# The features of x in a hybrid decoder trunk: the array made 64 bytes longer, with two starts inside it

## The chip, the cores and the metric

The kernel runs on one core of a Trainium2 chip. The metric is device microseconds of one execution. The core has TensorE (PE, with its weight loads shown as PEld), VectorE (DVE), ScalarE (ACT), GpSimd (POOL) and SyncE (SP). Its on-chip memory has 128 partitions; a tile's place is a byte offset that is the same in every partition.

## The reference

A trunk of two layers on 256 tokens of width 2048, in float32. Layer 0 normalises x, projects it with one matrix of 6144 columns, feeds a gated linear recurrence (RG-LRU) and a gated outer-product recurrence (HGRN2), projects the result, and ends with a squared-ReLU MLP of width 8192. Layer 1 has windowed attention in the place of the recurrences, and the same MLP.

```
proj = h @ w_in                                   # layer 0, one combined projection
mixed = concat([lru, hg]);   h = h + mixed @ w_out
h = h + square(relu(rms_norm(h) @ w1)) @ w2       # both layers
qkv = (h @ w_qkv)                                 # layer 1
h = h + dilated_attention(...) @ w_o
```

## The kernel before, in words

**Products in parts.** Every float32 operand is split into a high part (rounded to the chip's short float32 format, fp32r) and a low part (the remainder). A product is three matmuls: high by high, high by low, low by high. Weights arrive as tiles of 128 x 2048 (1 MB); `Weights` (lines 101 to 117) makes `hi` by a ScalarE copy (line 112) and `lo` by a VectorE subtraction (line 113). There are three buffers each of `raw`, `hi` and `lo`, used in turn. Weights that are sums or differences of two tiles go through `t1`/`t` and `s` (lines 138 to 166), which is how the later stages save matmuls.

**The array of x's features.** `bufa` (line 62) has 16 blocks of 128 features; block k holds 256 columns of the high part (one per token) and then 256 columns of the low part, so 512 words or 2048 bytes a block and 32768 bytes a partition. Layer 0 fills it while the weights of the first projection arrive (`fetch_first`, line 182). Two kinds of reader follow in layer 0. `tokens` (line 311, called by `tokens_group`, line 338) takes 128 x 128 slices of the features as the stationary operand and streams 512 columns of weights past them; the steps `v0 k0 v1 k1` of the order in line 1076 do this. `project` (line 346, by way of `direct`, line 230) takes a 128 x 128 slice of weights as the stationary operand and streams 256 columns of features; the steps `h`, `x` and `y` do this (`hgrn`, `lru_in`, `lru_out`).

**Later stages.** From layer 0's MLP on, `to_features` (line 668) writes the features of the new x to `bufa`, and `blocks` (line 605) reads slices of it through `feature` (line 597) as the stationary operand, with 512 columns of weights streamed. The other stationary arrays are `bufb`, `formx` and `formh`.

**Order.** All matmuls are tied into one chain (`mm`, line 195), so TensorE's order is that of the code. A scheduler places the rest; loads are fetched two units ahead (`unit`, line 185).

**Where tiles lie.** Pools are laid out one after the other. These are the byte offsets in a partition that the built program has, and where they fall in a block of 2048 and of 128 bytes:

| tile | bytes | offset | within 2048 | within 128 |
|---|---|---|---|---|
| constants (`cst`), `tab_`, `ones` | | 4224 to 6944 | | |
| `xall` (x by tokens) | 16384 | 6944 | 800 | 32 |
| `bufa` | 32768 | 23328 | 800 | 32 |
| `raw` (first of 3) | 8192 | 56096 | 800 | 32 |
| `hi` (first of 3) | 8192 | 80672 | 800 | 32 |
| `lo` (first of 3) | 8192 | 105248 | 800 | 32 |
| `bufb` | 32768 | 132384 | 1312 | 32 |
| `formx` | 16384 | 165152 | 1312 | 32 |
| `t1` / `s` | 8192 | 181536 / 189728 | 1312 | 32 |
| `formh` | 16384 | 197920 | 1312 | 32 |

A weight slice of 128 columns is 512 bytes and one of 512 columns is 2048 bytes; a stationary slice of features is 512 bytes. So before the change the two operands of every fp32r matmul start at offsets that differ by a multiple of 512 bytes.

Of the kernel before, what the change touches and what calls it, by code (L numbers as in the profile page):

```python
# [11 lines left out]
F32R = mybir.dt.float32r  # L12
# [8 lines left out]
P = 128  # L21
S = 256
D = 2048
KB = D // P
# [18 lines left out]
def trunk_kernel(ctx, tc, begin, xtok, cols, tab, masks, pos, fin, w_in, w_gate, w_out, w_qkv, w_o, w1, w2, out):  # L43
# [3 lines left out]
    act = pool("act")  # L47
# [11 lines left out]

    xall = act.tile([P, KB * S], F32, name="xall")  # L60
    xres = xall.rearrange("p (j d) -> p j d", j=2)
    bufa = act.tile([P, KB, 2 * S], F32R, name="bufa")

    units = []
    made = {}
# [15 lines left out]
    for step in ORDER.split():  # L81
        src, first, n = where[step[0]]
# [85 lines left out]
    def fetch_first():  # L168
        r = opening.tile([P, 14, WIDE], F32, name="first")
        e = wraw.tile([P, 2048], F32, name="raw")[:, :2 * WIDE].rearrange("p (k s) -> p k s", s=WIDE)  # L170
        homes = [r[:, k] for k in range(14)] + [e[:, k] for k in range(2)]
        nc.sync.dma_start(r[:, 0, :S], begin[:, 0, :S])
        nc.sync.dma_start(r[:, 0, S:], begin[:, 0, S:])
        for k in range(1, 4):
            nc.sync.dma_start(r[:, k], begin[:, k])
        for k in range(4, 16, 2):
            nc.sync.dma_start(r[:, k:k + 2] if k < 14 else e, begin[:, k:k + 2])
        for u in range(4):
            at[0] += 1
            w = made[u] = Weights(None, 0)  # L180
            for k in range(4 * u, 4 * u + 4):
                split_to(bufa[:, k], homes[k][:, :S], col("nmix0", k))
                w.split((k - 4 * u) * 512, 512, homes[k][:, S:])

    def unit(src, i):
# [52 lines left out]
    def split_to(dst, src, gain=None):  # L238
        if gain is None:
            h, l = dst[..., :S], dst[..., S:]  # L240
            A.copy(h, src)
            V.tensor_tensor(l, src, h.bitcast(F32), OP.subtract)
        else:
            A.activation(dst[:, :S], src, AF.Copy, scale=gain)
            V.scalar_tensor_tensor(dst[:, S:], src, gain, dst[:, :S].bitcast(F32),  # L245
                                   op0=OP.mult, op1=OP.subtract)

    c_ = cst.tile([P, NCOL], F32, name="c_")
    col = lambda n, i=0, w=1: c_[:, COLS[n][0] + i:COLS[n][0] + i + w]
# [86 lines left out]
        return ps  # L336

    def tokens_group(src, i0, rt=None, by_k=False, name="vg"):
        ps = tokens(src, i0, bufa, by_k)
        v = vgs.tile([P, 2, 512], F32, name=name)  # L340
        with urgent():
            for j in range(2):
                A.activation(v[:, j], ps[j], AF.Copy, scale=1.0 if rt is None else rt[:, j:j + 1])
        return v

    def project(src, i, mov):
        w = unit(src, i)
        p = pmm.tile([P, 512], F32, name="p")
        direct(p, w, [(k, mov[:, k], k == 0, k == KB - 1) for k in range(KB)])
        return p  # L350
# [85 lines left out]
    def hgrn(hd, vg, gg):  # L436
        u0 = 20 + (hd // 4) * 16 + (hd % 4) * 2
        oml = omlb[:, hd:hd + 1]
        qk = wk.tile([P, 2 * S], F32, name="qk", bufs=3)
        qp, kq = qk[:, :S], qk[:, S:]  # L440
        p = project(w_in, u0, bufa)
        z = normed(p, "hz", 4)
        lut(qp, z, AF.Sigmoid)
        V.scalar_tensor_tensor(qp, z, oml, qp, op0=OP.mult, op1=OP.mult)
        p = project(w_in, u0 + 1, bufa)
        z = normed(p, "hz", 4)
        f = wk.tile([P, S], F32, name="f", bufs=3)
        lut(f, z, AF.Sigmoid)
        lut(kq, z, AF.Sigmoid, scale=-1.0)
        V.tensor_scalar(f, f, oml, lb[:, hd:hd + 1], op0=OP.mult, op1=OP.add)  # L450
        pd = psc.tile([P, 2, P], F32, name="pd", bufs=1)
        for j in range(2):
            js = slice(j * P, j * P + P)
            T.matmul(pd[:, j], kq[:, js], qp[:, js], start=True, stop=True)  # L454
        st = wk.tile([P, 3, P], F32, name="st", bufs=3)
        V.tensor_tensor(st[:, :2], pd, ident[:, None, :].to_broadcast([P, 2, P]), OP.mult)
        stf = st[:, :2].rearrange("p a b -> p (a b)")
        V.tensor_tensor(qp, qp, f, OP.mult)
        c = 1
        tot = f  # L460
        while c <= 128:
            pl = psc.tile([P, 2, 64], F32, name="pl", bufs=2)
            if c == 128:
                plf = pl.rearrange("p j c -> p (j c)")
                T.matmul(plf, kq[:, :P], qp[:, P:], start=True, stop=True)  # L465
                A.copy(st[:, 2], plf)
                break
            for j in range(2):
                js = slice(j * P, j * P + P)
                T.matmul(pl[:, j], kq[:, js], halves(qp[:, js], c, True), start=True, stop=True)  # L470
            if c <= 16:
                lv = LEVELS.index(c)
                V.copy_predicated(halves(stf, c, True), msk[:, lv].rearrange("p (n c) -> p n c", c=c),
                                  pl.rearrange("p j (n c) -> p (j n) c", c=c))
            elif c == 32:
                for n in range(2):
                    ps_ = slice(64 * n, 64 * n + 32)
                    A.copy(st[ps_, :2, 64 * n + 32:64 * n + 64], pl[ps_, :, 32 * n:32 * n + 32])
            else:
                A.copy(st[:64, :2, 64:], pl[:64])  # L480
            n = S // (2 * c)
            tt = tot.rearrange("p (n two) -> p n two", two=2)
            both = bass.AP(tensor=qk.tensor, offset=qk.offset + c,
                           ap=[list(qk.ap[0]), [S - c, 2], [2 * c, n], [1, c]])
            fac = bass.AP(tensor=tot.tensor, offset=tot.offset,
                          ap=[list(tot.ap[0]), [1, 2], [2, n], [0, c]])
            V.tensor_tensor(both, both, fac, OP.mult)
            nt = wk.tile([P, n], F32, name=f"tot{n}", bufs=2)
            V.tensor_tensor(nt, tt[:, :, 0], tt[:, :, 1], OP.mult)
            tot = nt  # L490
            c *= 2
        vs = slice((hd % 4) * P, (hd % 4) * P + P)
        po = psc.tile([P, 2, P], F32, name="po", bufs=1)
        T.matmul(po[:, 0], st[:, 0], vg[:, 0, vs], start=True, stop=True)
        T.matmul(po[:, 1], st[:, 2], vg[:, 0, vs], start=True, stop=False)  # L495
        T.matmul(po[:, 1], st[:, 1], vg[:, 1, vs], start=False, stop=True)  # L496
        o = wk.tile([P, 2, P], F32, name="ho", bufs=2)
        hs = wk.tile([P, 2], F32, name="hs", bufs=2)
        for j in range(2):
            A.activation(o[:, j], po[:, j], AF.Square, accum_out=hs[:, j:j + 1])  # L500
        V.tensor_scalar(hs, hs, 1.0 / P, EPS, op0=OP.mult, op1=OP.add)
        hr = wk.tile([P, 2], F32, name="hr", bufs=2)
        rsqrt(hr, hs, 2)
        for j in range(2):
            V.scalar_tensor_tensor(o[:, j], po[:, j], hr[:, j:j + 1], gg[:, j, vs], op0=OP.mult, op1=OP.mult)
        pt = psc.tile([P, 2, P], F32, name="pt", bufs=1)
        for j in range(2):
            T.transpose(pt[:, j], o[:, j], ident)
        split_to(bufb[:, 8 + hd], pt.rearrange("p j c -> p (j c)"), col("gn", hd))
# [1 line left out]
    xc = wk.tile([P, 8, S], F32, name="xc", bufs=1)  # L511

    def lru_in(b):
        p = project(w_in, b, bufa)
        xp = wk.tile([P, S + 4], F32, name="xp", bufs=1)
        V.memset(xp[:, :4], 0.0)
        scaled(p, xp[:, 4:])
        A.activation(xc[:, b], xp[:, 4:], AF.Identity, bias=col("conv_b", b), scale=col("conv_w", 24 + b))
        for i in range(3):
            V.scalar_tensor_tensor(xc[:, b], xp[:, 1 + i:1 + i + S], col("conv_w", 8 * i + b), xc[:, b],  # L520
                                   op0=OP.mult, op1=OP.add)
        split_to(bufb[:, b], xc[:, b])
# [24 lines left out]
            V.tensor_tensor_scan(xc[:, b], gr[:, m], xc[:, b], 0.0, op0=OP.mult, op1=OP.add)  # L547

    def lru_out(b):
        p = project(w_in, 8 + b, bufa)  # L550
        y = tmp.tile([P, S], F32, name="z")
        scaled(p, y)
        q = wk.tile([P, S], F32, name="q", bufs=1)
        A.activation(q, y, AF.Square, scale=math.sqrt(0.044715))
        V.scalar_tensor_tensor(q, q, 1.0, y, op0=OP.add, op1=OP.mult)
        lut(q, q, AF.Sigmoid, scale=2.0 * math.sqrt(2.0 / math.pi))
        V.tensor_tensor(y, y, q, OP.mult)
        V.tensor_tensor(y, y, xc[:, b], OP.mult)
        split_to(bufb[:, b], y)
# [470 lines left out]
    for i, what in enumerate(ATTENTION):  # L1030
# [12 lines left out]
        else:  # L1043
            q, k = queries_keys(i, ((1, 0),) if not i else ())
# [24 lines left out]

LAST = 2  # L1070
EARLY = 12
BOUNDARY = 56
PRIO = 150
URGENT = 400
# [114 lines left out]
```

## Time and profile before

| what | value |
|---|---|
| median of 3 runs | 2133.09 us (2132.8 to 2133.53) |
| the profiled execution's own time | 2133.06 us |
| its span, first to last instruction | 2131.3 us |
| PE busy | 2120.9 us, 100% of the span, 10542 matmuls |
| PEld busy | 1797.6 us, 84% |
| DVE busy | 1788.8 us, 84% |
| ACT busy | 1378.2 us, 65% |
| DMA | 488.71 MB, mean 229 GB/s |
| granted TensorE clock | 0.999 |

A row of the groups reads: line, engine, operation, output and inputs by the program's names, shape, count, then busy us and the mean ns of one, then the engine's idle time just before them. PE matmuls overlap in the record, since each is shown from its start to the end of its results; the distance from one start to the next is what a matmul costs a full engine.

### The profile page before, as it was taken

To read this page: it belongs to the slowest core of one execution; us is meant where nothing else is said; L and a number is where in the kernel's file an instruction comes from. 1 tells how busy PE (TensorE), PEld (TensorE's weight loads), DVE (VectorE), ACT (ScalarE), POOL (GpSimd) and SP (SyncE) were. 2 spreads that over 40 slices of the span, in tenths; PEclk is the share of its full clock that TensorE was granted. 3 is DMA by queue.
4 is the path that set the end of the run, shared out by engine and by line. 5 is a ranking of instruction groups with operands and counts; after the bars stand their busy time and mean duration, and the time that the engine had idled before them with its cause. 6 is when DMAs were issued, how large, how long until landed. Compare 5 with 4: busy or idle time off the path is not lost.

```text
span 2131.3 us, 26730 instructions
## 1 busy us (share of the span) xinstructions
PE 2120.9 (100%) x10542; PEld 1797.6 (84%) x10542; DVE 1788.8 (84%) x1962; ACT 1378.2 (65%) x1543; POOL 66.8 (3%) x85
## 2 busy tenths in 40 slices
PE   9999999999999999999999999999999999999998
PEld 8989998888888888888888888888888888888886
DVE  7777888888888888888988797788897888888887
ACT  7445565776476567567666777776756765755764
POOL 0000000000000000000000000000000000000000
PEclk9999999999999999999999999999999999999999
DMA  8444446686777677677887767777767768777773
GB/s 336 162 162 158 161 148 224 206 269 233 227 237 253 230 240 253 227 241 231 270 279 218 241 199 247 254 247 228 246 237 253 236 212 269 238 234 227 271 225 146
DMA packets 69806, 488.71 MB, mean 229 GB/s; under 512 B 7808, under 2 KB 8320, under 8 KB 11952
## 3 DMA queue, kind: packets, MB, share of 16 engines
q1 hardware_dynamic: 58176, 410.96, 51.1%
q0 software_dynamic: 11216, 75.70, 18.3%
q8 instruction: 82, 1.34, 0.3%
q14 instruction: 44, 0.36, 0.0%
q10 hardware_dynamic: 288, 0.34, 0.0%
HBM read 482.78 MB, written 4.19 MB: 228 GB/s over the span
## 4 chain that ended last, share of the span: by engine, by line
PE 99%; DVE 0%; ACT 0%; DMA 0%; issue 0%; ACTq 0%; DVEq 0%; POOLq 0%
PE p L196 62%; PE po L196 14%; PE pd L196 13%; PE pt L196 5%; PE pl L199 2%; PE pl L470 1%; PE pl L196 0%; PE pd L199 0%; DMA ppi<-in_pos 0%; PE pd L454 0%; DVE lo L113 0%; ACT hi L112 0%; PE pl L465 0%; PE po L495 0%; PE po L496 0%
## 5 line engine op out<-in xcount | busy, mean ns | idle before, releaser
L113 DVE TENSOR_TENSOR lo<-raw,hi 128x2048 fp32r<-128x2048 f32 (+2 forms) x397 | 787.1, 1991 | 164.5 <-ACT hi L112 159.4
L112 ACT CAST hi<-raw 128x2048 fp32r<-128x2048 f32 (+2 forms) x397 | 657.3, 1671 | 335.1 <-PE p L196 175.5
L196 PE MATMUL p<-hi,bufa 128*128 128x512 f32 x1488 | 482.0, 394 | 0.0
L196 PE MATMUL p<-hi,bufb 128*128 128x512 f32 x1128 | 363.1, 391 | 0.0
L196 PEld LDWEIGHTS p<-hi,bufa 128*128 128x128 f32 x1488 | 279.2, 188 | 57.3 <-DVE bufa L245 0.5
L113 DVE TENSOR_TENSOR lo<-s,hi 128x2048 fp32r<-128x2048 f32 (+1 forms) x164 | 285.9, 1753 | 28.6 <-ACT hi L112 27.6
L112 ACT CAST hi<-s 128x2048 fp32r<-128x2048 f32 (+1 forms) x164 | 242.7, 1480 | 98.2 <-DVE s L164 54.2
L196 PE MATMUL p<-lo,bufa 128*128 128x512 f32 x744 | 287.6, 390 | 0.2 <-DVE lo L113 0.2
L196 PEld LDWEIGHTS p<-hi,bufb 128*128 128x128 f32 x1128 | 211.7, 188 | 43.7
L196 PE MATMUL p<-lo,bufb 128*128 128x512 f32 x564 | 219.5, 389 | 0.0
L196 PE MATMUL p<-bufa,hi 128*128 128x256 f32 x1024 | 193.2, 287 | 0.0
L196 PEld LDWEIGHTS p<-lo,bufa 128*128 128x128 f32 x744 | 139.9, 188 | 28.0 <-DVE lo L113 0.7
L196 PEld LDWEIGHTS p<-bufa,hi 128*128 128x128 f32 x1024 | 161.2, 191 | 0.2
L196 PE MATMUL p<-bufa,lo 128*128 128x256 f32 x512 | 146.5, 286 | 0.0
L112 ACT CAST hi<-t 128x2048 fp32r<-128x2048 f32 x41 | 78.5, 1914 | 99.6 <-PE p L196 91.1
L113 DVE TENSOR_TENSOR lo<-t,hi 128x2048 fp32r<-128x2048 f32 x41 | 94.0, 2292 | 55.4 <-ACT hi L112 55.0
L196 PEld LDWEIGHTS p<-lo,bufb 128*128 128x128 f32 x564 | 105.9, 188 | 21.5
L196 PE MATMUL p<-hi,formh 128*128 128x512 f32 x368 | 120.7, 391 | 0.0
L196 PE MATMUL p<-hi,formx 128*128 128x512 f32 x352 | 115.9, 390 | 0.0
L196 PE MATMUL po<-hi,bufb 128*128 128x512 f32 x320 | 103.7, 390 | 0.0
L196 PEld LDWEIGHTS p<-bufa,lo 128*128 128x128 f32 x512 | 98.0, 191 | 0.0
L164 DVE TENSOR_TENSOR s<-s,raw 128x1024 f32<-128x1024 f32 x82 | 96.4, 1216 | 0.1
(319 smaller groups left out, 3292.4 us busy)
## 6 DMA issues: line engine op xcount, KB each, us to landing
raw<-in_w SPq DMA_DIRECT2D x224, 1024.0 KB, 6.1
raw<-in_w_in SPq DMA_DIRECT2D x44, 1024.0 KB, 4.8
raw<-in_w_qkv SPq DMA_DIRECT2D x42, 1024.0 KB, 6.9
t<-in_w SPq DMA_DIRECT2D x32, 1024.0 KB, 4.9
t<-in_w POOLq DMA_DIRECT2D x32, 1024.0 KB, 8.7
s<-in_w POOLq DMA_DIRECT2D x17, 1024.0 KB, 8.4
raw<-in_w_out SPq DMA_DIRECT2D x15, 1024.0 KB, 4.8
raw<-in_w_o SPq DMA_DIRECT2D x14, 1024.0 KB, 7.7
```

The source lines that it names most:

```text
L112: a = A.copy(h, w)
L113: v = V.tensor_tensor(l, w, h.bitcast(F32), OP.subtract)
L164: V.tensor_tensor(s, s, held["c"][:, at:at + 1024], OP.add)
L196: chain[:] = [after(T.matmul(*args, **kw), chain)]
L199: chain[:] = [after(T.transpose(out_, in_, ident), chain)]
L470: T.matmul(pl[:, j], kq[:, js], halves(qp[:, js], c, True), start=True, stop=True)
```

## The change

The array gets 16 words (64 bytes) more per partition, and two views of it are made: `bufx` starts at its first word, `bufa` 16 words later. Layer 0's fill and its readers (`fetch_first`, `tokens_group`, `hgrn`, `lru_in`, `lru_out`) use `bufx`. `to_features` and `feature`, that is every later stage, keep the name `bufa` and with it the upper view.

```diff
-    bufa = act.tile([P, KB, 2 * S], F32R, name="bufa")
+    bufa_ = act.tile([P, KB * 2 * S + APART], F32R, name="bufa")
+    bufx, bufa = (bufa_[:, o:o + KB * 2 * S].rearrange("p (k c) -> p k c", k=KB) for o in (0, APART))
...
-                split_to(bufa[:, k], homes[k][:, :S], col("nmix0", k))
+                split_to(bufx[:, k], homes[k][:, :S], col("nmix0", k))
...
-        ps = tokens(src, i0, bufa, by_k)
+        ps = tokens(src, i0, bufx, by_k)
...
-        p = project(w_in, u0, bufa)
+        p = project(w_in, u0, bufx)
...
-        p = project(w_in, u0 + 1, bufa)
+        p = project(w_in, u0 + 1, bufx)
...
-        p = project(w_in, b, bufa)
+        p = project(w_in, b, bufx)
...
-        p = project(w_in, 8 + b, bufa)
+        p = project(w_in, 8 + b, bufx)
...
+APART = 16
```

In the built program the instructions of all five engines, their order and the semaphores they wait for are the same as before. What differs is addresses: `xall`, the constants and layer 0's view of x stay where they are; every tile from `raw` on, and the later stages' view of x, lies 64 bytes further up. So in layer 0 the start of x and that of the weights differ by a multiple of 512 bytes plus 64; in the later stages the operands of each fp32r matmul stand to each other as before.

## The prediction

> **What bounds the kernel now.** I read the page's busy table first, then the chain of work that ended last, then who PE waited for.
>
> ```profile
> span 2131.3 us, 26730 instructions
> ...
> PE 2120.9 (100%) x10542; PEld 1797.6 (84%) x10542; DVE 1788.8 (84%) x1962; ACT 1378.2 (65%) x1543; POOL 66.8 (3%) x85
> ...
> PE 99%; DVE 0%; ACT 0%; DMA 0%; issue 0%; ACTq 0%; DVEq 0%; POOLq 0%
> ```
>
> PE is busy all through the span and carries 99% of the chain. Busy is a weak word here, since matmuls overlap in the record, so the list of PE's own waits matters more:
>
> ```profile
> PE po L255 <- DVE xp L516: 1.1, 1, 1.1
> PE p L196 <- DVE lo L113: 0.2, 1, 0.2
> PE pl L465 <- DVE qk L487: 0.2, 1, 0.2
> PE pt L196 <- DVE xall L939: 0.2, 1, 0.2
> ```
>
> Columns: total us, times, longest. These four are the whole list, 1.7 us. So no load, no split and no eviction sets the time: it is the sum of the distances between matmul starts. Two windows of the timeline (start, us, instruction) show that distance where nothing disturbs it. In layer 0, with x streamed:
>
> ```profile
> 214.16 0.40 PE L196 MATMUL p<-bufa,hi 128*128 128x256 f32 x2
> 214.40 0.28 PE L196 MATMUL p<-bufa,lo 128*128 128x256 f32 x1
> ...
> 216.20 0.28 PE L196 MATMUL p<-bufa,lo 128*128 128x256 f32 x1
> 216.32 0.28 PE L196 MATMUL p<-bufa,hi 128*128 128x256 f32 x1
> ```
>
> From 214.16 to 216.32 stand six groups of three, 18 matmuls: 2.16 us / 18 = 120.0 ns each. In the MLP, with weights streamed:
>
> ```profile
> 643.49 0.39 PE L196 MATMUL p<-hi,bufa 128*128 128x512 f32 x1
> 643.72 0.39 PE L196 MATMUL p<-lo,bufa 128*128 128x512 f32 x1
> ...
> 648.48 0.39 PE L196 MATMUL p<-lo,bufa 128*128 128x512 f32 x1
> 648.70 0.39 PE L196 MATMUL p<-hi,bufa 128*128 128x512 f32 x1
> ```
>
> From 643.49 to 648.70 stand 23 matmuls: 5.21 us / 23 = 226.5 ns each. The difference, 106.5 ns for 256 columns, is 0.416 ns a column; what is left, 120.0 - 106.5 = **13.5 ns, is paid by every matmul whatever its width**. That fixed part is the only thing in this profile on which an address could act with effect, because everything else has slack.
>
> **The change part by part.** It adds no instruction, removes none, moves none, and adds no wait. It changes places only, in three ways, and I cost them one by one.
>
> *1. Everything from `raw` on lies 64 bytes higher (absolute place).* For DVE and ACT the trace has the same operation on tiles in different places: `raw` starts 800 bytes into a block of 2048, `s` 1312.
>
> ```profile
> L113 DVE TENSOR_TENSOR lo<-raw,hi 128x2048 fp32r<-128x2048 f32 x287 | 656.5, 2290 | 134.7 <-ACT hi L112 130.1 <-PE pt L196 2.3 <-PE p L196 1.1
> L113 DVE TENSOR_TENSOR lo<-s,hi 128x2048 fp32r<-128x2048 f32 x82 | 187.6, 2288 | 23.4 <-ACT hi L112 22.4
> ```
>
> ```profile
> L112 ACT CAST hi<-raw 128x2048 fp32r<-128x2048 f32 x287 | 548.3, 1913 | 249.7 <-PE p L196 137.8 <-PE pd L196 48.9 <-PE po L196 48.7
> L112 ACT CAST hi<-s 128x2048 fp32r<-128x2048 f32 x82 | 156.8, 1912 | 43.8 <-PE pd L196 18.5 <-PE po L196 16.4 <-PE pt L196 4.6
> ```
>
> 2290 and 2288 ns, 1913 and 1912 ns: a place 512 bytes away moves them by at most 2 ns in 2290, 0.1%. I take nothing. Even 1% more on all of DVE (18 us) would stay under cover: PE is what hides it, DVE has 16% of the span idle, and the waits on it above sum to 1.7 us. For PE the same test is the stationary tile: `bufb` and `formx` begin 512 bytes further into a 2048-byte block than `bufa`.
>
> ```profile
> L196 PE MATMUL p<-hi,bufb 128*128 128x512 f32 x482 | 155.2, 391 | 0.0
> L196 PE MATMUL p<-hi,bufa 128*128 128x512 f32 x448 | 145.1, 392 | 0.0
> ...
> L196 PE MATMUL p<-hi,formx 128*128 128x512 f32 x128 | 42.0, 389 | 0.0
> ```
>
> 391, 392 and 389 ns in the stretch of layer 0's out projection and MLP (356 to 1030 us): no effect of the stationary tile's place beyond the odd matmuls around transposes. Counting boundaries says the same: a read of 2048, 1024 or 512 bytes that starts 32 bytes into a block of 128 crosses as many boundaries of 128 bytes as one that starts 96 bytes in, and the place within 64 bytes is unchanged. Cost: 0, from bounds of 0 to 0.1% of DVE and ACT, both hidden.
>
> *2. Weights land 64 bytes higher.*
>
> ```profile
> q1 hardware_dynamic: 58176, 410.96, 51.1%
> ...
> raw<-in_w SPq DMA_DIRECT2D x224, 1024.0 KB, 6.1
> ```
>
> A load lands 6.1 us after its issue, and no DMA stands in PE's list of waits; that lead is the cover. Cost: 0. The Trainium skill, "DMA: Bandwidth & Descriptors", section "How a descriptor splits into AXI transactions", speaks against the change here: transactions begin on 256-byte boundaries, and bytes ahead of a start still cost beats. A row of 8192 bytes that starts 32 bytes past a boundary would be 257 beats, one that starts 96 past it 259, an estimate of 0.8% more (the page tells it of reads; this is the written side). No run here shows it yet, and at 51.1% it would be hidden.
>
> *3. In layer 0, x and the weights no longer start a multiple of 512 bytes apart.* This is the only relation between two operands of an fp32r matmul that changes. Its size is bounded by the matmuls that touch `bufx`, all before 356 us:
>
> ```profile
> L196 PE MATMUL p<-bufa,hi 128*128 128x256 f32 x1024 | 193.2, 287 | 0.0
> L196 PE MATMUL p<-bufa,lo 128*128 128x256 f32 x512 | 146.5, 286 | 0.0
> L196 PE MATMUL p<-hi,bufa 128*128 128x512 f32 x256 | 78.9, 396 | 0.0
> L196 PE MATMUL p<-lo,bufa 128*128 128x512 f32 x128 | 47.8, 394 | 0.2 <-DVE lo L113 0.2
> ```
>
> 1024 + 512 + 256 + 128 = 1920 matmuls. Before the change both reads of each matmul (its own stream, and the next one's weights that load beside it) always start at the same place modulo 512 bytes, so the trace has no row of another relation: the price must be bounded. Below: the 13.5 ns go entirely, 1920 x 13.5 = 25.9 us gained. Above: they double, 25.9 us lost. I take 0, for this reason: the load beside a matmul reads 512 bytes while the stream reads 1024 or 2048, so the distance between the two reads sweeps over hundreds of bytes within each matmul. A start 64 bytes off only shifts that sweep. And the relation does differ already by 0, 512, 1024 or 1536 modulo 2048 without a trace in 391 / 392 / 389 ns.
>
> The page "TensorE: Matmul & The Clock Gate" of the Trainium skill, section "Part 2", step 1, says that the stream and the weight load have two independent read ports, so that loading weights takes nothing from the running matmul; by that rule part 3 is worth exactly 0. Its section on the warm start-to-start distance gives N / 2.4 + 2.5 ns, an estimate of 109.2 ns for 256 columns; the trace has 120.0, so measurement and page differ by 10.8 ns, which the page doesn't account for. Were that the price of the relation, the estimate would be 1920 x 10.8 = 20.7 us, inside the bound above.
>
> **The sum.** 0 + 0 + 0, made against the profiled execution: 2131.3 us of span and 1.8 us around it, 2133.1 us, which is also the median of the runs (2133.09).
>
> **The rivals.**
>
> *Faster: the fixed part is a collision of equal starts.* The stream and the weight load begin together and at the same place modulo 512 bytes; if that costs both a detour, 64 bytes apart frees them. For it: 13.5 ns independent of width looks like something at the start or during the load, and the load beside it is always 128 columns wide. Against it: the sweep, and that DVE and ACT rows don't feel places. It would reach the 1920 matmuls of layer 0 alone. Whole: 2133.1 - 25.9 = 2107.2 us. I price it at half, 13 us, since two streams that still share the memory should keep some of it: 2120.1 us.
>
> *Slower: the settled rhythm is lost.* After a transpose or a small matmul the next few are further apart and then settle:
>
> ```profile
> 1155.85 0.63 PE L196 MATMUL pt<-hi,formx 128*128 128x512 f32 x2
> 1156.32 0.39 PE L196 MATMUL pt<-lo,formx 128*128 128x512 f32 x1
> 1156.54 0.63 PE L196 MATMUL pt<-hi,formx 128*128 128x512 f32 x2
> 1157.01 0.39 PE L196 MATMUL pt<-lo,formx 128*128 128x512 f32 x1
> 1157.23 0.62 PE L196 MATMUL pt<-hi,formx 128*128 128x512 f32 x2
> ```
>
> From 1155.85 to 1157.23 are 6 matmuls in 1.38 us, 230.0 ns each, 3.5 more than when settled. So the fixed part does depend on how the stream and the load stand to each other in time, and by the same token may depend on how they stand in place. If layer 0 stays in the unsettled state all through, 1920 x 3.5 = 6.7 us: 2139.8 us. It decides from 2.2 ns a matmul on (4.3 us / 1920), in the `project` steps between 51 and 330 us. Against it: those rows settle whatever the tile.
>
> **How the numbers follow.** About 0.2%, 4.3 us, is what a measurement of this kernel can tell from no change. Nothing beyond that: 0.56, since each of the parts is 0 by its nearest row, though part 3 by argument rather than by a row. The faster rival: 0.24. The slower rival: 0.20; the unsettled rows make it real, and nothing says on which side a new relation falls. The forecast's own range is 2129 to 2137. For 8 in 10 I take in the faster rival down to its half price, 2120, and the slower one up to 2140; left out are a gain of more than half of the fixed part (about 0.08) and a loss beyond the unsettled rhythm (about 0.08).
>
> **What would show each step right or wrong.** In the profile after: parts 1 and 2 hold if DVE's and ACT's mean ns of the splits stay at 2290 and 1913 and loads land after 6.1 us. Part 3 is read from the same 256-column window: 120.0 ns from start to start means no effect, 113 the faster rival at half, 123.5 or more the slower one. The MLP window must read 226.5 ns again, since its operands keep their relation; if it moves, absolute place does matter and the step on it failed, with the other 8622 matmuls (10542 - 1920) behind it. The time would then be off by far more than the range. What would make the prediction wrong is a row of PE that depends on place at a finer grain than 512 bytes, which no row of before can show.

## The result, and the profile after

The changed kernel takes 2129.18 us, the median of 19 runs (2128.4 to 2129.88), against 2132.74 us for 19 runs of the kernel before (2132.12 to 2133.53): a ratio of 0.9983, with a 95% interval of 0.9976 to 0.999. That is 3.56 us or 0.17%: inside the predicted range, and below the 0.2% that the prediction took as the least that a measurement can tell from no change. But that bound was too wide: each set of 19 spreads over 1.5 us at most, and the two sets don't touch. The forecast was no effect, and there is a small, real gain. The profiled execution took 2128.4 us, at a granted clock of 0.999 as before.

The page, in the parts that were read before:

```profile
span 2126.6 us, 26730 instructions
...
PE 2115.9 (99%) x10542; PEld 1792.4 (84%) x10542; DVE 1788.8 (84%) x1962; ACT 1378.2 (65%) x1543; POOL 66.7 (3%) x85
...
q1 hardware_dynamic: 58176, 410.96, 51.2%
...
PE 98%; DVE 1%; ACT 1%; DMA 0%; issue 0%; ACTq 0%; DVEq 0%; POOLq 0%
...
raw<-in_w SPq DMA_DIRECT2D x224, 1024.0 KB, 6.1
```

Against before, PE's busy time is 5.0 us less (2120.9) and the span 4.7 us less; DVE and ACT are busy for the same 1788.8 and 1378.2 us. PE still carries the chain. Its waits, all of them (total us, times, longest), come to 1.9 us, where they were 1.7:

```profile
PE po L256 <- DVE xp L517: 1.1, 1, 1.1
PE pl L471 <- DVE qk L488: 0.4, 1, 0.4
PE pl L466 <- DVE qk L488: 0.2, 1, 0.2
PE pt L197 <- DVE xall L940: 0.2, 1, 0.2
```

So no wait went: the matmuls themselves follow each other faster. The groups of the window 0 to 351 us show where:

```profile
L197 PE MATMUL p<-bufa,hi 128*128 128x256 f32 x1024 | 187.8, 283 | 0.0
L197 PE MATMUL p<-bufa,lo 128*128 128x256 f32 x512 | 144.7, 283 | 0.0
L197 PE MATMUL p<-hi,bufa 128*128 128x512 f32 x256 | 78.8, 395 | 0.0
L197 PE MATMUL p<-lo,bufa 128*128 128x512 f32 x128 | 48.1, 396 | 0.1
```

The 256-column groups fell from 193.2 and 146.5 us, 287 and 286 ns each; the 512-column ones stayed (78.9 and 47.8). In the timeline (start, us, instruction), where every group of three took 0.36 us before, a stretch now settles in one of two rhythms. The first:

```profile
54.92 0.39 PE L197 MATMUL p<-bufa,hi 128*128 128x256 f32 x2
55.14 0.28 PE L197 MATMUL p<-bufa,lo 128*128 128x256 f32 x1
...
57.64 0.39 PE L197 MATMUL p<-bufa,hi 128*128 128x256 f32 x2
57.86 0.28 PE L197 MATMUL p<-bufa,lo 128*128 128x256 f32 x1
57.98 0.39 PE L197 MATMUL p<-bufa,hi 128*128 128x256 f32 x2
```

From 54.92 to 57.98 stand 27 matmuls: 3.06 us / 27 = 113.3 ns. And the second, further on:

```profile
207.86 0.40 PE L197 MATMUL p<-bufa,hi 128*128 128x256 f32 x2
208.10 0.28 PE L197 MATMUL p<-bufa,lo 128*128 128x256 f32 x1
...
209.16 0.28 PE L197 MATMUL p<-bufa,lo 128*128 128x256 f32 x1
209.27 0.40 PE L197 MATMUL p<-bufa,hi 128*128 128x256 f32 x2
```

12 matmuls in 1.41 us, 117.5 ns. There are 38 stretches of 18 or more such matmuls with nothing between them. Read nine matmuls at a time, after the first six of each, 18 of these stretches run at 113.3 ns throughout and 20 at 117.8. In the MLP nothing moved:

```profile
638.49 0.39 PE L197 MATMUL p<-hi,bufa 128*128 128x512 f32 x1
638.72 0.39 PE L197 MATMUL p<-lo,bufa 128*128 128x512 f32 x1
...
643.48 0.39 PE L197 MATMUL p<-lo,bufa 128*128 128x512 f32 x1
643.70 0.39 PE L197 MATMUL p<-hi,bufa 128*128 128x512 f32 x1
```

23 matmuls in 5.21 us, 226.5 ns, as before.

Below, the **start distance** of a kind of matmul is its mean over the whole trace: from each start to the next, leaving out distances of 150 ns and more for 256 columns and 260 ns and more for 512, which hold a wait or a transpose. For the change, counted so (of 512 columns in layer 0, 365 are left before and 367 after):

| start distance, ns | count | before | after | difference, us |
|---|---|---|---|---|
| layer 0, 256 columns, x streamed | 1468 | 119.80 | 116.08 | -5.46 |
| layer 0, 512 columns, x stationary | 367 | 227.84 | 229.40 | +0.57 |
| later, 512 columns, `bufa` stationary | 2831 | 227.44 | 227.51 | +0.20 |

The sum is -4.7 us, which is the difference of the two profiled executions (2133.06 - 2128.4 = 4.66). The medians are only 3.56 us apart, since after's profiled execution was the fastest of its 19 (0.78 below its median) and before's lay 0.32 above its own.

### The profile page after: what moved, and what is told of

Same layout as the page of the kernel before. It is cut to its first block, busy times and chain, and to the rows that moved or that the text cites. A ratio compares the mean times of both kernels' runs of the same rounds, so it can differ in the third digit from the quotient of the medians.

```text
span 2126.6 us, 26730 instructions
## 1 busy us (share of the span) xinstructions
PE 2115.9 (99%) x10542; PEld 1792.4 (84%) x10542; DVE 1788.8 (84%) x1962; ACT 1378.2 (65%) x1543; POOL 66.7 (3%) x85
## 3 DMA queue, kind: packets, MB, share of 16 engines
q1 hardware_dynamic: 58176, 410.96, 51.2%
q0 software_dynamic: 11216, 75.70, 18.6%
## 4 chain that ended last, share of the span: by engine, by line
PE 98%; DVE 1%; ACT 1%; DMA 0%; issue 0%; ACTq 0%; DVEq 0%; POOLq 0%
PE p L197 62%; PE po L197 14%; PE pd L197 13%; PE pt L197 5%; PE pl L200 2%; PE pl L471 1%; PE pl L197 0%; PE pd L200 0%; ACT hi L113 0%; DMA ppi<-in_pos 0%; DVE lo L114 0%; PE pd L455 0%; ACT L226 0%; DVE xc L548 0%; ACT gi L226 0%
## 5 line engine op out<-in xcount | busy, mean ns | idle before, releaser
L197 PE MATMUL p<-bufa,hi 128*128 128x256 f32 x1024 | 187.8, 283 | 0.0
```

Of the source, the lines that this page charges most:

```text
L197: chain[:] = [after(T.matmul(*args, **kw), chain)]
```

## The experiments

Two theories stood at the start. *Distance*: what counts is how far apart the starts of x and of the weights lie. *Place*: what counts is where the weights, or x, lie by themselves. All edits are to the changed kernel unless said otherwise; "distance" is weights minus x, in bytes, modulo 512, and it is 0 before and 64 after.

### e1: weights 64 bytes up, x up with them

```diff
-... for o in (0, APART))
+... for o in (16, 16))
```

> The array is 64 bytes longer and everything from the weights' buffers on lies 64 bytes higher, but layer 0 too keeps x at the upper end, so every pair of operands stands to each other as before. Theory A (what counts is how far apart x and the weights start): the 256-column matmuls of layer 0 are 119.8 ns apart again, as before the change (116.1 after it), and the time is that of before, 2132.7 us, ratio 1.000 within 0.0007. Rival B (the absolute place of the weights counts): 116.1 ns stays and the time is 2129.2 us, ratio 0.998.

2133.52 us (2132.89 to 2134.27) against 2132.93 for before beside it, ratio 1.0003 (0.9994 to 1.0012). Start distance 119.82 ns in layer 0. The timeline of e1:

```profile
214.16 0.40 PE L197 MATMUL p<-bufa,hi 128*128 128x256 f32 x2
...
215.84 0.28 PE L197 MATMUL p<-bufa,lo 128*128 128x256 f32 x1
215.96 0.28 PE L197 MATMUL p<-bufa,hi 128*128 128x256 f32 x1
```

15 matmuls in 1.80 us: 120.0 ns again. The weights lie where they lie after the change, and the gain is gone, so their place alone doesn't make it. Nor does the place of x alone, which the change leaves where it was. It is the distance between the two.

### e2: the later stages 64 bytes apart too

```diff
+... for o in (0, 0))
```

> Both views at the lower end, so x and the weights start 64 bytes off in every stage. Theory A: layer 0 as after the change (256 columns 116.1 ns apart, 512 columns 229.4 instead of 227.8), and the later stages' 512-column matmuls on this array, some 2830 undisturbed ones, go from 227.5 to about 229.0 ns: 2129.2 + 2830 x 1.6 ns = 2133.7 us, ratio to before 1.0005. Rival B (absolute place): no stage but layer 0 changes, 2129.2 us.

2135.06 us (2134.39 to 2135.56), ratio 1.001 (1.0001 to 1.0019); layer 0 at 116.38 ns as after the change, the later 512-column matmuls on `bufa` at 229.25. The MLP window of e2:

```profile
640.67 0.39 PE L197 MATMUL p<-hi,bufa 128*128 128x512 f32 x1
640.90 0.39 PE L197 MATMUL p<-lo,bufa 128*128 128x512 f32 x1
...
645.71 0.39 PE L197 MATMUL p<-lo,bufa 128*128 128x512 f32 x1
645.94 0.39 PE L197 MATMUL p<-hi,bufa 128*128 128x512 f32 x1
```

23 matmuls in 5.27 us: 229.1 ns against 226.5. 2831 x 1.74 ns (229.25 - 227.51) is 4.9 us, of the 5.7 by which e2 and the change differ, each against before beside it (+2.13 and -3.56); layer 0's 116.38 in the place of 116.08 ns adds 0.4. The same 64 bytes that help 256 streamed columns cost 512 streamed ones, so two views are needed for the gain: one for each kind.

### e3 and e4: 128 and 512 bytes apart

```diff
-APART = 16
+APART = 32        (e3; e4: 128)
```

> Layer 0 has x 128 bytes below the weights' relation instead of 64; later stages as before. Theory A: the 256-column distance is another one again, under 119.8 ns and not that of 64 bytes; I expect 110 to 118 ns, so 2121 to 2131 us. Rival B (absolute place within 128 bytes): the weights stand at 32 within 128 as before the change, so 119.8 ns and 2132.7 us.

One run: 2133.54 us. 256 columns at 119.42 ns, 512 on x at 232.60. The expected gain did not come: the 256-column figure is back near that of distance 0, while the 512-column one is the slowest so far, so distance still acts. More distance is not more gain.

> Layer 0 has x 512 bytes below, that is again a multiple of 512 from the weights; later stages as before. Theory A with the distance counted modulo 512 bytes: 119.8 ns and 2132.7 us. Theory A2 (any distance other than that of before frees the two reads): 116 ns or less, 2129 us or less.

One run: 2133.29 us; 119.80 and 228.03 ns, those of distance 0. A whole 512 bytes is no distance at all.

### e5 to e8: a finer map

Each kernel places the two halves of x at two distances and the later view at a third, so that one run gives three:

```diff
+    low, high, bufa = (bufa_[:, o:o + KB * 2 * S].rearrange("p (k c) -> p k c", k=KB)
+                       for o in (APART - 8, APART - 4, APART - 112))
+
+    class Two:
+        def __getitem__(self, at):
+            return (low if at[1] < KB // 2 else high)[at]
+
+    bufx = Two()
...
+APART = 128
```

The words in this diff are those of e5 (32, 16 and 448 bytes); the others have 24, 12, 64 (e6), 48, 28, 8 (e7) and 112, 20, 96 (e8).

> Three distances in one kernel, read stage by stage from the distances between matmul starts: in layer 0 the first 8 blocks of x lie 32 bytes below the weights' relation and the last 8 blocks 16 bytes; the later stages' view lies 448 bytes below, that is 64 above modulo 512. So far 256 columns cost 119.8 ns at 0 and 512 bytes, 116.1 at 64 and 119.4 at 128; 512 columns cost 227.5, 229.3 and 232.6. Theory A1 (the price repeats every 128 bytes): 32 and 16 bytes lie between, 116 to 120 ns. Theory A2 (it repeats only every 512 bytes): no bound from the others; under 116 is possible. Later stages, 64 above: A1 says 229 ns as at 64 below.

> First 8 blocks of x 96 bytes below, last 8 blocks 48 bytes; later stages' view 256 bytes below. A1 (period of 128 bytes): 96 bytes costs what 32 bytes below or above cost, 116 to 120 ns for 256 columns, 48 bytes 116 to 117; later stages at 256 bytes 227.5 ns for 512 columns. A2 (period of 512): later stages at 256 bytes differ from 227.5 ns.

> First 8 blocks of x 192 bytes below, last 8 blocks 112 bytes; later stages' view 32 bytes below. A1 (period of 128 bytes): 192 costs what 64 costs, 116.1 ns, with its two rhythms of 113 and 118; A2 (period of 512): another number. Later stages at 32 bytes: between 227.5 and 229.3 ns if the price moves smoothly.

> First 8 blocks of x 448 bytes below, that is 64 above modulo 512; last 8 blocks 80 bytes below; later stages' view 384 bytes below, 128 above modulo 512. A1 (period of 128 bytes): 448 costs what 64 costs, 116.1 ns for 256 columns; later stages at 384 bytes 227.5. A2 (period of 512): other numbers, and if the order of the two reads counts, 64 above differs from 64 below.

Measured, one run each: 2150.59, 2132.64, 2148.13 and 2148.55 us, against 2132.03 for before. The time follows the later view: 448, 32 and 384 bytes cost the later matmuls 233.36, 233.08 and 232.60 ns, and 256 bytes 227.44, the best. For e5, 2831 x (233.36 - 227.44) = 16.8 us, of 18.6 measured. So for 512 columns distances repeat every 256 bytes (256 reads like 0 and 512, 448 like 192, 384 like 128), and not every 128: 192 bytes gives 233.2 ns where 64 gives 229.4, and 128 gives 232.6 where 0 gives 227.9. Of the two periods that had been proposed, 128 is refuted, and 512 isn't the shortest. For 256 columns the period is less sure: 448 bytes gave 117.7 ns, 192 gave 117.1 and 64 gave 116.1, and 256 bytes wasn't tried. Nor is the price smooth: 32 bytes was expected between the 227.5 ns of 0 and the 229.3 of 64, and costs 233.08.

### e9 and e10: steps of 4 and 8 bytes around 64

The same edit with 18, 14, 60 words (e9) and 17, 15, 2 (e10).

> So far the price repeats every 256 bytes: 512 columns cost 227.4 ns at 256 as at 0, and 232.6 at 384 as at 128. At 64 bytes the 256-column matmuls have two rhythms, about 113.3 and 117.7 ns, and each stretch between small matmuls settles in one of them. Here the first 8 blocks of x lie 72 bytes below, the last 8 blocks 56. If the place counts in steps of 16 bytes or more, 72 costs what 64 costs, 116 ns with both rhythms, and 56 what 48 costs, 118.8. If it counts finer, the shares of the two rhythms change; the best case is 113.3 ns throughout. Later stages' view 240 bytes below (16 above): 512 columns between 228 and 234 ns; under 227.4 only if the price is not lowest at 0.

> First 8 blocks of x 68 bytes below, last 8 blocks 60; the same two theories as for 72 and 56: steps of 16 bytes give 116 ns at 68 and 118.8 at 60, a finer grain other shares of the rhythms of 113.3 and 117.7 ns. Later stages' view 8 bytes below: 227.5 ns if steps of 16 bytes count, else toward the 228.1 of 16 bytes.

2139.68 and 2152.56 us, one run each, before 2132.94. Around 64 bytes (116.1 ns) stand 120.5, 121.5, 118.4 and 119.9 ns at 56, 60, 68 and 72; the later view at 8 bytes costs 233.15 where 0 costs 227.4 and 228.1 at most was expected. The effect changes from one 4-byte word to the next.

### e13 to e15: the second half of the period

The same edit with 40, 36, 0 words (e13), 56, 52, 0 (e14) and 60, 44, 0 (e15).

> First 8 blocks of x 160 bytes below, last 8 blocks 144; later stages as before. The map so far for 256 columns: 0: 119.8, 16: 117.3, 32: 118.4, 48: 118.8, 56: 120.5, 64: 116.1, 80: 119.2, 96: 117.9, 112: 118.1, 128: 119.4, 192: 117.1 ns. Theory: a settled rhythm takes what it takes by where the load crosses the stream, so any value from 113 to 121 is possible, and 64 stays the lowest; rival: one of the unmeasured distances locks all stretches at 113.3 ns.

> First 8 blocks of x 224 bytes below, last 8 blocks 208; later stages as before. As for 160 and 144: 113 to 121 ns for 256 columns, 64 stays the lowest at 116.1, or one of these locks at 113.3. 512 columns in layer 0: all above 227.9.

> First 8 blocks of x 240 bytes below, last 8 blocks 176; later stages as before. As for 160 and 144: 113 to 121 ns for 256 columns, or one of these locks at 113.3. 512 columns at 240 in layer 0: 229.0, which is what the later stages gave at 240.

2131.44, 2130.98 and 2132.82 us, one run each, before 2132.62. The map, from all runs so far (ns, layer 0, ten of the distances). Where x lies at two distances, the first nine matmuls of each half are left out, since they still follow the other half; with them 144 bytes reads 115.1 in the place of 114.3:

| bytes apart | 0 | 16 | 48 | 64 | 112 | 128 | 144 | 160 | 192 | 240 |
|---|---|---|---|---|---|---|---|---|---|---|
| 256 columns, x streamed | 119.8 | 117.3 | 118.8 | 116.1 | 118.1 | 119.4 | 114.3 | 119.7 | 117.1 | 117.6 |
| 512 columns, x stationary | 227.9 | 228.1 | 232.6 | 229.4 | 231.3 | 232.6 | 233.1 | 233.9 | 233.2 | 230.7 |

For 512 columns 0 (or 256) is the lowest of all; for 256 columns it is among the worst. 144 bytes was the best of all for 256 columns, in half of x, where 64 had been expected to stay the lowest. One more expectation failed: 240 bytes was to cost 229.0 ns for 512 columns, as the later stages gave in e9 with x and the weights at the same places (228.96), and it cost 230.7 in layer 0. So these places don't fix the time alone, and what else enters isn't known.

### e16 to e18: 144 bytes for all of x, and the place within 64 bytes

e16 takes the change with 36 words. There the weights shift by 144 bytes, where in e13 they had shifted by 512. e17 has the distance of e16 with the shift of e13; e18 has the change's own distance with that shift.

```diff
+APART = 36                                        (e16, for o in (0, APART))
+... for o in (APART - 36, APART))                 (e17, APART = 128)
+... for o in (APART - 16, APART))                 (e18, APART = 128)
```

> The changed kernel with 36 words (144 bytes) in the place of 16: layer 0 keeps x 144 bytes below, later stages as before. If the half of x measured at 144 bytes speaks for all of it: 1468 undisturbed 256-column matmuls at 114.3 instead of 119.8 ns, -8.1 us, and layer 0's 367 with 512 columns at 233.1 instead of 227.9, +1.9 us: 2132.7 - 6.2 = 2126.5 us, ratio to before 0.9971, and faster than the change itself by 2.7 us. Rival: the rhythm of 113.3 ns came from the other half's state, and the whole lies at 116 to 118 ns, 2129 to 2132 us.

2136.16 us (2135.72 to 2137.3) against 2133.17: ratio 1.0014 (1.0005 to 1.0023). A miss by 9.7 us. The timeline of e16:

```profile
54.93 0.40 PE L197 MATMUL p<-bufa,hi 128*128 128x256 f32 x2
55.17 0.28 PE L197 MATMUL p<-bufa,lo 128*128 128x256 f32 x1
...
56.25 0.28 PE L197 MATMUL p<-bufa,lo 128*128 128x256 f32 x1
56.37 0.40 PE L197 MATMUL p<-bufa,hi 128*128 128x256 f32 x2
```

12 matmuls in 1.44 us, 120.0 ns, and 119.72 over layer 0.

> All of x 144 bytes below the weights in layer 0, as in the run before (119.7 ns for 256 columns), but with the array 512 bytes longer, so that the weights lie 512 bytes up and x 368, which are the places of the half that ran at 114.3 ns. Theory 'place' (absolute places count as well as the distance): 114.3 ns for all, about 2126.5 us, ratio 0.997. Theory 'history' (at 144 bytes there are several settled rhythms, and the half entered the fast one from the rhythm of the half before it): 119.7 ns as in the run before, about 2135 us, ratio 1.001.

2128.29 us (2127.5 to 2128.86) against 2132.83: ratio 0.9977 (0.9968 to 0.9986). In e17 the fast rhythm, which the change has in some stretches only, holds in most; 24 matmuls in 2.72 us, 113.3 ns:

```profile
57.99 0.39 PE L197 MATMUL p<-bufa,hi 128*128 128x256 f32 x2
58.21 0.28 PE L197 MATMUL p<-bufa,lo 128*128 128x256 f32 x1
...
60.71 0.39 PE L197 MATMUL p<-bufa,hi 128*128 128x256 f32 x2
```

Its mean is 114.3 ns, but the 512-column matmuls on x pay 233.30, 5.5 ns more than before. By these two the distances sum to 6.0 us less than before, and the profiled execution gained 4.7 (2133.06 - 2128.32). PE's waits grew meanwhile: they sum to 3.4 us, where they were 1.7 before. The largest new one is for a weight tile's high part:

```profile
PE p L197 <- ACT hi L113: 1.1, 1, 1.1
```

The distance is that of e16; what differs is that both operands lie 368 bytes further up, x at 16 and the weights at 32 within 64 bytes, where in e16 they start at 32 and 48. So place counts beside distance. By e1 and the next run, made at distances 0 and 64, it is the place within 64 bytes that counts.

> All of x 64 bytes below the weights, as in the changed kernel, but with the array 512 bytes longer, so that both lie higher by 448 bytes. Distance alone counts: 116.1 ns for 256 columns with both rhythms, about 2129.2 us. Absolute places count: another number.

One run: 2128.64 us; 116.41 and 229.43 ns, with both rhythms (18 of the 38 long stretches at 113.3 ns, 20 at 117.8), as after the change. Shifts of both by whole multiples of 64 bytes change next to nothing: 0.02 ns from before to e1, 0.3 ns from the change to e18. Of the 38 stretches, 33 have the same rhythm in the change, in e2 and in e18, where about 10 would if each were drawn by a coin. So the rhythm of a stretch isn't drawn anew in each execution. This also qualifies the map: at distances that are no multiple of 64, it holds for the one place of the weights at which it was measured.

e17 is the fastest kernel that computes the whole of the reference, but its interval and the change's overlap, so it is not shown to be better than the change.

### e11 and e12: what the second operand of the distance is

Both are edits to the kernel before. e11 puts 64 bytes between the high and the low parts of the weights, so that the loads of `lo` lie 64 bytes off those of `hi`, which stay where they were. The arrays behind `lo` (`bufb`, `formx`, `formh`) move up with it, so in the later stages `hi` stands to them at a new distance too. It was to tell whether a matmul pays by the load beside it or by its own weights.

```diff
+    gap = pool("gap")
     wlo = pool("wlo", 3)
...
+    V.memset(gap.tile([P, 16], F32, name="gap"), 0.0)
```

> The kernel before, with a gap of 64 bytes (and one memset of 16 words) ahead of the buffers of the weights' low parts. In layer 0's projections each block makes three matmuls: x's high part and then its low part on the high weights, then x's high part on the low weights. x and the high weights stand to each other as before, x and the low weights 64 bytes off. Theory 'beside' (a stream collides with the next weights that load while it runs): it is the second of the three whose distance leaves 120 ns, since the low weights load beside it. Rival 'own' (the stream and the weights that it runs on): it is the third. No effect in any of the three, 119.8 ns each, would speak against both. The time is no measure here, since later stages get new relations too (their high weights against the other arrays): slower, by up to 25 us.

One run: 2177.77 us, 45 us slower than before (2132.94), where 25 us at most had been expected. In layer 0 the three matmuls of a group have 118.02, 117.62 and 118.21 ns: they share one rhythm, so neither reading is told apart. The loss comes later. The groups of e11 from 356 to 1060 us:

```profile
L197 PE MATMUL p<-hi,bufb 128*128 128x512 f32 x494 | 162.1, 397 | 0.0
L197 PE MATMUL p<-hi,bufa 128*128 128x512 f32 x448 | 147.2, 396 | 0.0
```

391 and 392 ns before. Start distances of the later stages rose from 227.4 to 231.91 ns with `bufa` stationary, from 227.0 to 234.36 with `bufb`, and from 227.1 to 234.34 and 234.00 with `formh` and `formx`. 2904, 2511, 1008 and 1056 matmuls times these (4.5, 7.4, 7.3, 6.9 ns) give 46 us; layer 0 gives back 1.4.

e12 shortens the load: in layer 0's `direct`, all but the first and last block of features use 32 of the 128 columns of weights. It leaves out three quarters of these products, so the matmuls get narrower with the loads (32 rows of output in the place of 128); the stream past them stays 256 columns.

```diff
-            h, l = w.part(blk * P, P)
+            n = P if first or last else 32
+            h, l = w.part(blk * P, n)
+            o = p[:n]
...          (the three matmuls write to o)
```

> The kernel before (x and weights a multiple of 512 bytes apart), but in the projections of layer 0 all 256-column matmuls between the first and the last block of a projection use only 32 of the 128 weight columns, so three quarters of those outputs' sums are left out; x streams as before. Theory 'load' (the fixed part is what the weight load beside a stream takes from it): the load is a quarter as long, so the fixed part falls from 13.3 to about 3.3 ns, 256 columns 110 ns apart. Rival 'swap' (a fixed price of changing weights): 120 ns as before.

One run: 2127.45 us, before 2132.62. The weight loads of e12 in layer 0 (PEld, mean ns of one after the bar):

```profile
L196 PEld LDWEIGHTS p<-bufa,hi 128*32 128x32 f32 x896 | 96.6, 108 | 6.6
...
L196 PEld LDWEIGHTS p<-bufa,hi 128*128 128x128 f32 x128 | 20.0, 189 | 0.4
```

A load takes 108 ns instead of 189, yet the start distance only falls from 119.8 to 117.42 ns. The rhythms of 113 and 117 ns appear with x and the weights at distance 0, others between them too; the fast one:

```profile
102.76 0.39 PE L196 MATMUL p<-bufa,hi 128*32 128x256 f32 x2
...
103.78 0.39 PE L196 MATMUL p<-bufa,hi 128*32 128x256 f32 x2
```

Nine matmuls in 1.02 us, 113.3 ns. So the load beside a matmul isn't the whole of its fixed part, for which 110 ns was expected. The 120 ns of a fixed price for changing weights weren't seen either. That the load bears on the fixed part at all is likely but not shown, since the matmuls changed with their loads.

## Why the prediction was wrong, point by point

**What bounds the kernel** held: the time is the sum of the start distances, and the change of the profiled time is the change of that sum (-4.7 by both). But the 13.5 ns "paid by every matmul whatever its width" aren't one fixed price: the change took 3.7 ns from the 256-column matmuls of layer 0 and added 1.6 to the 512-column ones.

**Part 1, absolute place, taken at 0**, held for the change: DVE's and ACT's splits read as before.

```profile
L114 DVE TENSOR_TENSOR lo<-raw,hi 128x2048 fp32r<-128x2048 f32 x287 | 656.3, 2290 | 134.4 <-ACT hi L113 130.6 <-PE pt L197 2.4
L113 ACT CAST hi<-raw 128x2048 fp32r<-128x2048 f32 x287 | 548.3, 1913 | 249.6 <-PE p L197 140.0 <-PE pd L197 48.9 <-PE po L197 48.7
```

The MLP's 226.5 ns stand, and e1 shows the 64 bytes alone to be worth nothing. But it held because 64 bytes leave the place within 64 unchanged; e16 against e17 (119.72 and 114.3 ns at one distance) shows that TensorE does feel place. The prediction noted that it stays, and gave it no weight.

**Part 2, the landing place, taken at 0**, held: loads land after 6.1 us as before, and q1's share is 51.2% where it was 51.1%. The Trainium skill, "DMA: Bandwidth & Descriptors", section "How a descriptor splits into AXI transactions", has transactions start on 256-byte boundaries. By the estimate made from it in the prediction, 0.4 points more were due (0.8% of 51.1). No such rise is seen: e17 and e18, whose weight rows start as far past a 256-byte boundary as before's, read 51.4 and 51.5%, more than the change, so a difference of that size comes without it.

**Part 3, the distance, taken at 0, is the step that failed.** Measured, it is worth 4.9 us: -5.5 on the 256-column matmuls of layer 0 and +0.6 on its 512-column ones. That the median still lies inside the forecast's own range of 2129 to 2137, by 0.18 us, is luck: the effect is small, and nothing in the working said so. Two reasons were given. The first was the sweep: since the reads pass over hundreds of bytes within a matmul, a start 64 bytes off should only shift the sweep. e2, e1 and e4 refute it: 64 bytes apart, together, and 512 apart give 116.4, 119.8 and 119.8 ns in layer 0 with the same instructions. The second was the row of 391, 392 and 389 ns for stationary tiles 512 bytes apart. By e4 and e6, 256 and 512 bytes are whole periods, so this row compared equal cases; it could not have shown an effect. It was read as evidence of none, although the text itself said that a grain finer than 512 bytes would be invisible there. The rule quoted beside it, of "TensorE: Matmul & The Clock Gate", section "Part 2", step 1 of the Trainium skill, is that loading weights takes nothing from the running matmul. What the prediction drew from it, that part 3 is worth exactly 0, isn't borne out: between e1 and e2 the distance alone moved the matmuls by 3.4 ns. Whether the load takes that time isn't shown; e12, with shorter loads and narrower matmuls, moved them by 2.4 ns.

**The faster rival** had the right cause in part: the fixed part depends on the relative start of the two operands, in layer 0 alone. Its price was wrong. Half of 13.5 ns on 1920 matmuls was 13 us; measured are 3.7 ns on the 256-column ones (the window's 113 ns holds in some stretches, 117.5 in others) and a loss on the 512-column ones, 4.9 us in all. "Equal starts collide" is not the mechanism either: for 512 columns equal starts are the best of all tried.

**The slower rival** had its sign for a part: 1.6 ns more on the 512-column matmuls of layer 0, 0.6 us, below the 2.2 ns from which it was to decide, and on a fifth of the matmuls.

**What stays open.** What in the chip makes a matmul's fixed part depend on these places isn't settled: the two simple readings, the load beside and the matmul's own weights, were not told apart by e11, and e12 fits neither end and changed two things at once. Nor is it known what decides which rhythm a stretch falls into: the change and e18 have both, mostly in the same stretches, and e17 mostly the fast one.

## What to carry to other kernels

Where TensorE is the bound and each matmul has new weights, read the distance from start to start in an undisturbed window, and vary by a few words how far apart the streamed and the stationary operand lie: here that was worth from 0.2% gained (layer 0 alone) to 2% lost (e11, 64 bytes between two pools), and the best distance differed between 256 and 512 streamed columns. Added constants or pools can shift this by accident, so an edit that adds no work can still move the time. And before a row counts as evidence of no effect, ask whether the cases in it differ in the thing that might act: places that are whole periods apart show nothing.

## What the runs showed of the hardware

At several places a TensorE-bound stretch with 256 streamed columns settled in one rhythm and kept it: 120.0 ns in the kernel before, 113.3 or 117.8 ns in the change, e2 and e18. Other places gave other means, up to 121.5 ns at 60 bytes (e10), so these three aren't all. The distance from start to start depends on operand places: it changed with single 4-byte words (116.1 ns at 64 bytes, 118.4 at 68), repeated every 256 bytes of distance for 512 columns (227.44 ns at 256 and at 0), and shifts of both operands by 64 and 448 bytes moved it by 0.3 ns at most. For 512 columns it ran from 227.0 to 234.4 ns. A weight load of 32 columns took 108 ns and one of 128 columns 189, though the narrower matmuls that went with the short loads came only 2.4 ns sooner. The granted clock was 0.998 or 0.999 in all of these runs.
